# A trunk layer with planned side work: w_ada streamed through the place of keys and values, w_attn_proj sums made where they are used

## The chip, the cores and the metric

The kernel runs on one core of a Trainium2 chip. Its engines are TensorE (PE; its weight loads are listed as PEld), VectorE (DVE), ScalarE (ACT), GpSimd (POOL) and SyncE (SP), which here only issues transfers. Every engine works through its own instructions in order and waits for others through semaphores; transfers run on 16 DMA engines. The metric is the device time of one execution in microseconds, as the median of several runs, and less is better.

## The reference

One layer of a decoder trunk on x (2048 x 1024), float32:

```python
mod = silu(c) @ w_ada + b_ada                    # 3 x 1024: shift, scale, gate
u = x * (1 + scale) + shift
q, k, v, a_gate, p_in, p_gate, m_a, m_p = split(u @ w_in)
a = (sliding_window_gqa_with_sinks(q, k, v, bias) * silu(a_gate)) @ w_attn_proj
p = (group_linear(causal_pool(p_in), w_pool_mix) * pool_scale * silu(p_gate)) @ w_pool_proj
y = ((sigmoid(m_a) * a + sigmoid(m_p) * p) @ w_out) * (1 + gate)
out = layer_norm(alpha * x + y)
```

There are 16 query heads and 2 key heads of 64, a window of 128 and a bias by distance.

## The kernel before, in words

**Products.** A float32 matrix is split into a high half (rounded to the type of one fast pass, ACT) and a low half (the rest, one subtraction, on DVE or POOL: `low`, L124), and `mm3` (L130) multiplies high by high, high by low and low by high. The big products take a 2 x 2 block scheme with seven products instead of eight (`Quad`, L256): both operands need sums of their blocks. On the moving side these are the "sets" B11, T1, T2, B21, T3, B22, T4 and B12, each [128, 4, 2, 512] with high and low halves; on the weight side a quad holds three tiles `W` (L153, two buffers) and one `A22`. `Quad.load` fetches blocks and makes the first sum on POOL (L276), `mid` makes two more (L283, L284) and fetches a block over one that is used up (L285), `late` one more (L292). The eight products of w_attn_proj have their weight sums made ahead, by `weight_sums` (L229) in the second gate phase, into HBM (`wq_d`), and load them from there (`number` is set, L268 to L271, L281, L290).

**Stages.** The 2048 rows go in two halves of 1024. (1) The head (L962 to L1033): w_ada times silu(c) gives shift, scale and gate in `mod`; PE makes shift from `wadat` (`modulation_mm`, L979), DVE makes scale from `wada` by a multiply with a running sum (`modulation`, L954). Tile by tile, x is modulated on ACT and made into sets, and each tile is multiplied into the first two quads' open products. (2) First gate phase: one quad for keys and values and 16 for the four gates (`gate_quads`, L942), two quads to a group. (3) First attention, 64 steps, a head pair and a block of 128 rows each. (4) and (5): the same for the second half. (6) The mixing phases ("mix"): w_attn_proj and w_pool_proj for the first half, both for the second, then w_out with the layer norm.

**What sets the order.** A planner orders instructions on each engine by its own estimate of time; calls through `pe`, `act`, `dve`, `pool`, `sp` (L83) keep the order of the program, all matmuls among them. Side work is hung on "ticks": `ring` (L392) calls the hooks of a tick after every product of 12 matmuls, `steps` (L411) turns a start and offsets into ticks (14 to a group of two quads). Side work of the gate phases: `fold_parts` (L900) multiplies w_pool_mix into a part of w_in, in halves, and stores it for the attention; `sums_to` (L194) fetches two tiles, works on them, stores them and their block sums; in the first gate phase these are the sets of the second half of x, in the second the rows of w_out times 1 + gate. It takes its two tiles from `spare`, a rotation of two 512 KB buffers shared with the folds, with `weight_sums` and with the builds of sets. `bias_rows` (L548) lays out the attention bias with 32 small POOL instructions.

**Ends of attention.** From step 51 the next phase's first two quads are loaded, split (`early_hi`, `early_lo`) and multiplied (`fill_one`, L756) beside the last steps, and its sets are built from `raw` tiles. PSUM has four `mm` banks; two of them hold the last pooled inputs until `pool_diff` (L656) has read them.

## Time and profile before

| what | us |
|---|---|
| median of 3 runs | 1969.79 (1968.75 to 1978.54) |
| profiled execution, its own time | 1969.13 |
| its span | 1967.4 |
| busy: PE, DVE, POOL, ACT | 1763.7, 1321.0, 1020.0, 943.3 |
| granted TensorE clock, mean | 0.961 |

In the profile's rows, `L55` stands for every instruction issued through the ordered engines, so tiles tell more than lines: `mm`, `lg`, `pv`, `pt` are PSUM banks, `w_set` a split weight, `W` and `A` a quad's weight blocks, `sig` a gate, `st_hi` and `st_lo` a fold's result. A row of the timeline gives start, duration, engine, line, operation, output and input; in brackets stands how long the engine had been idle before it and what ended that. A row of the waits names who waited for whom, the total, the times and the longest.

### The profile page before, as it was taken

The page shows a single profiled execution, that of the slowest core. Times are in us where ns is not written, and L with a number is a line of the kernel's source. Part 1 is how long each engine was busy: PE and PEld are TensorE (multiplying, and loading weights), DVE is VectorE, ACT ScalarE, POOL GpSimd, SP SyncE. Part 2 cuts the span into 40 slices and gives each one's busy share as a digit, 9 for nine tenths or more (in the row PEclk, how much of TensorE's full clock was granted, in tenths as well). Part 3 has the DMA queues.
Part 4 walks back from the last instruction along what each step waited for, and adds up shares of the span by engine and source line. Part 5 has one row for each costly group of instructions (what it writes and reads, how often), then busy time and mean ns, then how long its engine had stood idle before and what let it go on. Part 6 is the DMA issues. An engine that isn't in the chain of part 4 may idle for free. (4 is left out here: it accounts for less than half of the span.)

```text
span 1967.4 us, 25174 instructions
## 1 busy us (share of the span) xinstructions
PE 1763.7 (90%) x8248; PEld 1458.6 (74%) x8248; DVE 1321.0 (67%) x2252; ACT 943.3 (48%) x1945; POOL 1020.0 (52%) x908
## 2 busy tenths in 40 slices
PE   4589799989999997887899999999969989988996
PEld 3478687768888886666688888888758768766775
DVE  5565555354687888765544447787867886888776
ACT  2443333333777776422333357777734344333443
POOL 3464746541366777766533314667632751576452
PEclk9789999999999998898899999999979999999998
DMA  6352746366354444565533344444467686675442
GB/s 230 129 203 93 230 149 213 135 218 163 121 162 130 149 157 169 201 208 198 182 102 124 105 137 124 150 150 143 152 216 249 204 279 208 221 237 200 139 140 95
DMA packets 144147, 335.18 MB, mean 170 GB/s; under 512 B 19072, under 2 KB 23184, under 8 KB 144016
## 3 DMA queue, kind: packets, MB, share of 16 engines
q1 hardware_dynamic: 118112, 253.29, 40.3%
q0 software_dynamic: 20512, 67.15, 9.1%
q10 hardware_dynamic: 5392, 13.14, 1.9%
q8 instruction: 65, 1.06, 0.2%
q14 instruction: 66, 0.54, 0.1%
HBM read 224.43 MB, written 112.23 MB: 171 GB/s over the span
## 5 line engine op out<-in xcount | busy, mean ns | idle before, releaser
L55 PE MATMUL mm<-set_B,w_set 128*128 128x512 f32 x3240 | 817.5, 401 | 73.3 <-DVE w_set L125 22.0
L55 PEld LDWEIGHTS mm<-set_B,w_set 128*128 128x128 f32 x3240 | 612.1, 192 | 211.1 <-DVE w_set L125 30.0
L55 PE MATMUL lg<-set_T,w_set 128*128 128x512 f32 x2088 | 529.5, 404 | 77.6 <-DVE w_set L125 40.2
L55 PEld LDWEIGHTS lg<-set_T,w_set 128*128 128x128 f32 x2088 | 401.6, 195 | 179.6 <-DVE w_set L125 50.8
L125 DVE TENSOR_TENSOR w_set<-W,w_set 128x1024 fp32r<-128x1024 f32 x166 | 248.4, 1497 | 164.2 <-ACT w_set L314 149.6
L314 ACT CAST w_set<-W 128x1024 fp32r<-128x1024 f32 x166 | 174.4, 1051 | 278.0 <-PE mm L55 186.0
L55 PE MATMUL mm<-set_T,w_set 128*128 128x512 f32 x1080 | 272.2, 400 | 2.9 <-DVE w_set L55 2.9
L55 PEld LDWEIGHTS mm<-set_T,w_set 128*128 128x128 f32 x1080 | 205.5, 193 | 46.6 <-DVE w_set L55 3.7
L365 POOL TENSOR_TENSOR p<-p,u 128x512 f32<-128x512 f32 x58 | 85.3, 1473 | 157.9 <-DVE u L364 157.6
L292 POOL TENSOR_TENSOR W<-W 128x512 f32<-128x512 f32 x50 | 67.0, 1341 | 149.9 <-DVE w_set L125 138.8
L283 POOL TENSOR_TENSOR W<-W 128x512 f32<-128x512 f32 x50 | 78.1, 1561 | 117.1 <-DVE w_set L125 109.7
L55 ACT ACTIVATE L<-L,nm 128x257 f32<-128x257 f32 (+1 forms) x256 | 127.4, 500 | 10.6 <-DVE nm L55 3.7
L55 DVE TENSOR_TENSOR o<-pv,o 64x128 f32<-64x128 f32 x256 | 72.1, 282 | 77.1 <-ACT o L55 74.4
L55 DVE CUSTOM_DVE_ANT_0 L<-lg,bt,nsink 128x256 f32<-128x256 f32 (+1 forms) x256 | 111.6, 473 | 7.8 <-DMA bt<-e_rep 2.0
L276 POOL TENSOR_TENSOR W<-W,A 128x512 f32<-128x512 f32 x50 | 69.1, 1383 | 72.8 <-DMA W<-in_win_dram 33.9
L55 DVE TENSOR_SCALAR L<-L,sm 128x256 f32<-128x256 f32 (+1 forms) x128 | 97.2, 759 | 0.0
L55 ACT ACTIVATE L<-L,sm 128x256 f32<-128x256 f32 (+1 forms) x128 | 64.4, 503 | 54.0 <-DVE sm L55 53.8
L55 DVE TENSOR_TENSOR ptl<-pt,pth 128x512 fp32r<-128x512 f32 (+1 forms) x128 | 85.6, 669 | 1.5 <-ACT pth L55 1.4
L55 POOL TENSOR_TENSOR w_set<-W,w_set 128x1024 fp32r<-128x1024 f32 x14 | 33.7, 2405 | 98.5 <-ACT w_set L55 65.0
L284 POOL TENSOR_TENSOR W<-W 128x512 f32<-128x512 f32 x50 | 81.2, 1624 | 6.1 <-DMA W<-in_win_dram 3.5
L55 ACT COPY o<-pv 64x256 f32<-64x256 f32 x128 | 47.4, 370 | 76.4 <-PE pv L55 75.4
L125 DVE TENSOR_TENSOR set_T<-spare,set_T 128x1024 fp32r<-128x1024 f32 (+1 forms) x48 | 61.4, 1281 | 31.7 <-ACT set_T L180 31.6
(172 smaller groups left out, 2631.0 us busy)
## 6 DMA issues: line engine op xcount, KB each, us to landing
W<-in_win_dram SPq DMA_DIRECT2D x102, 256.0 KB, 3.4
w_set<-wmix_d SPq DMA_DIRECT2D x32, 512.0 KB, 5.9
A<-in_win_dram SPq DMA_DIRECT2D x34, 256.0 KB, 3.3
wa<-in_wada_dram SPq DMA_DIRECT2D x32, 256.0 KB, 3.8
ag_d<-sig SPq DMA_DIRECT2D x32, 256.0 KB, 3.4
pg_d<-sig SPq DMA_DIRECT2D x32, 256.0 KB, 3.4
ma_d<-sig SPq DMA_DIRECT2D x32, 256.0 KB, 2.4
mp_d<-sig SPq DMA_DIRECT2D x32, 256.0 KB, 2.9
```

The source lines that it names most:

```text
L55: return lambda *args, **kw: self.tc.keep_in_program_order(op(*args, **kw))
L125: engine.tensor_tensor(dst, src, as32(hi), ALU.subtract)
L276: nc.gpsimd.tensor_tensor(x[:, 1, :], x[:, 2, :], self.a22, ALU.add)
L283: nc.gpsimd.tensor_tensor(x[:, 1, :], x[:, 1, :], x[:, 0, :], ALU.subtract)
L284: nc.gpsimd.tensor_tensor(x[:, 2, :], x[:, 0, :], x[:, 2, :], ALU.subtract)
L292: nc.gpsimd.tensor_tensor(x[:, 0, :], x[:, 0, :], x[:, 1, :], ALU.subtract)
L314: nc.scalar.copy(by_two(hi), raw)
L365: nc.gpsimd.tensor_tensor(p5, p5, u2, ALU.add)
```

## The change

- **Head.** `head` and `places` are new. The tiles of `wadat` and `wada` come in one load each, into six places that lie where keys (`kk`) and values (`vv`) will stand later, instead of five half-size buffers. Tiles 0 and 4 are fetched and modulated, then the first two quads' weights; then for each i the sets of tiles i and 4 + i are made, the next two tiles are fetched and modulated, and only then are the products of tile i issued. `bias_rows` runs here instead of at tick 7 of the third group.
- **First gate phase.** `fold_parts` comes in five steps of one tick each (fetch, split, fold and fetch, split, fold), with the low half on DVE instead of POOL. The eight rows of w_ada for the gate come through `spare`, two every 28 ticks, instead of all from tick 92 on.
- **Second gate phase.** `weight_sums` and `wq_d` go; the sums of w_out start at tick 9 + 24.5 i with a stretch of 1.8 instead of 18 + 25.5 i with 1.1; the gate's rows are written in the first group instead of the second.
- **w_attn_proj.** Its quads make their sums on POOL like all others.
- **Attention.** The first low half of the next phase's weights goes to POOL, a step later; T1 is split three steps after its load; the four early products come in the order T1, B11, B11, T1 instead of T1, B11, T1, B11; the last two pool differences come one step earlier.

```diff
     class Quad:
         def load(self, ph, own):
             self.w, self.a22 = ph.weights(), ph.last(own)
-            x, made = self.w, self.number is not None
-            if made:
-                nc.sync.dma_start(x[:, 0, :], self.srcs[0][:, 0:CH])
-                nc.sync.dma_start(x[:, 1, :], wq_d[self.number, 0])
-                nc.sync.dma_start(x[:, 2, :], wq_d[self.number, 2])
-                nc.sync.dma_start(self.a22, self.srcs[1][:, CH:])
-                return
+            x = self.w
...
         def early_lo(x, which):
             hi, lo = pre[x, which]
-            low(dve, by_two(lo), nxt_group[x].first(), by_two(hi))
+            low(dve if x or which else pool, by_two(lo), nxt_group[x].first(), by_two(hi))
...
             if n < 64:
                 if n % 2 == 0:
                     opened.append([bank(), bank(), None, None])
-                    product(opened[x][1], pair(x, 0)[1], "T1", True)
-                else:
-                    product(opened[x][0], pair(x, 0)[0], "B11", True)
+                k = (n - 60) % 3 == 0
+                product(opened[x][k], pair(x, 0)[k], "T1" if k else "B11", True)
...
+            for at, x, which in ((57, 0, 0), (60, 1, 0), (62, 0, 1), (64, 1, 1)):
...
-                if n % U == 5 + 2 * st and (j, st) in sums:
+                if n % U == 4 + (j + 1 < KT) + 2 * st and (j, st) in sums:
                     pl = pool_diff(j, sums.pop((j, st)), accs.pop(("mix", j, st)))
...
             if n in (26, 42):
-                build(ph, "T1", n // 42, nxt_store, eng=(act, pool), raw=ph.weights()[:, 0:2])
+                t1_raw = ph.weights()[:, 0:2]
+                nc.sync.dma_start(t1_raw, nxt_store["T1"][n // 42])
+            if n in (29, 45):
+                split_set("T1", 2 * (n // 45), t1_raw, 2, eng=(act, pool))
...
     def fold_parts(ph, g):
+        m, r, w = [], [], []
+        def fetch(half):
+            if half == 0:
+                r.append(ph.c("mr"))
+                nc.sync.dma_start(r[0], mix[g])
+            r.append(ph.spare())
+            nc.sync.dma_start(r[-1], wpt[g, half])
+        def split(half):
...
+            w[:] = ph.split(), ph.split()
+            nc.scalar.copy(w[0], r[-1])
+            low(nc.vector, w[1], r[-1], w[0])
...
+        return (
+            (0, lambda: fetch(0)),
+            (1, lambda: split(0)),
+            (2, lambda: (fold(0), fetch(1))),
+            (3, lambda: split(1)),
+            (4, lambda: fold(1)),
+        )
...
+    def gate_modulation(ph, m, cb):
+        wa = []
+        def fetch():
+            wa.append(ph.spare())
+            nc.sync.dma_start(wa[0], wada[m])
+        def work():
             nc.vector.tensor_tensor_reduce(
+                wa[0], wa[0], cb, 1.0, mod[:, m : m + 1], ALU.mult, ALU.add, mod[:, m : m + 1]
             )
+        return (0, fetch), (3, work)
...
+    def head(ph, places):
...
+        bias_rows(ph)
         sums = bank("pv")
+        xs = {}
+        def fetch(k):
+            wt, wa = place(), place()
+            nc.sync.dma_start(wt, wadat[k])
+            nc.sync.dma_start(wa, wada[KT + k])
+            if k < 4:
+                xs[k] = (ph.spare(),)
+                nc.sync.dma_start(xs[k][0], xt[0, k])
+            else:
+                xs[k] = ph.p("b21"), ph.p("b22")
+                for h, x in enumerate(xs[k]):
+                    nc.sync.dma_start(x, cols(xt[0, k], h))
+            for i in range(KT):
+                mm(sums[:, k : k + 1], wt[:, i * P : (i + 1) * P], ct[:, i : i + 1], ...)
+            m = KT + k
+            nc.vector.tensor_tensor_reduce(
+                wa, wa, cb, 1.0, mod[:, m : m + 1], ALU.mult, ALU.add, mod[:, m : m + 1]
+            )
...
+            for x in xs[k]:
+                nc.scalar.activation(x, x, AF.Identity, bias=mod[:, k : k + 1], scale=mod[:, m : m + 1])
...
+        fetch(0)
+        fetch(4)
+        for q in groups[0]:
+            q.load(ph, False)
...
+        for i in range(4):
+            make_sets(i)
+            if i + 1 < 4:
+                fetch(i + 1)
+                fetch(i + 5)
             for w, (a, b, _, _) in zip(starts, opened):
                 product(a, w[0], "B11", True, i, i + 1)
                 product(b, w[1], "T1", True, i, i + 1)
...
         for g in range(4):
-            for half, f in enumerate(fold_parts(ph, g)):
-                at(2 * g, 2 * half, f)
+            steps(hooks, groups, 28 * g, fold_parts(ph, g))
...
-        at(2, 7, lambda: bias_rows(ph))
...
         for i in range(8):
-            steps(hooks, groups, 92, [(2.6 * i, lambda i=i: modulation(ph, 2 * KT + i, cb, lambda: ph.c("wa")))])
+            steps(hooks, groups, 28 * (i // 2) + 22 + i % 2, gate_modulation(ph, 2 * KT + i, cb))
...
-        hooks[(1, 2)] = [gate_rows]
+        hooks[(0, 2)] = [gate_rows]
...
-            steps(hooks, groups, 6 + 25.5 * i, weight_sums(ph, (wap[2 * i], wap[2 * i + 1]), i))
...
-                1.1,
+                1.8,
             )
-            steps(hooks, groups, 18 + 25.5 * i, todo)
+            steps(hooks, groups, 9 + 24.5 * i, todo)
...
+    def places():
+        big = kvp.tile([P, 4 * (P + 2 * CH)], F32, tag="kk", name="head_kk")
+        small = kvp.tile([P, 2 * (2 * NB + 1) * P], F32, tag="vv", name="head_vv")
+        return [t[:, i * D : (i + 1) * D] for t, n in ((big, 4), (small, 2)) for i in range(n)]
...
+        started = head(ph, places())
+        kk = kvp.tile([P, 2, 2, P + 2 * CH], F32R, tag="kk", name="kk")
+        vv = kvp.tile([P, 2 * NB + 1, 2, P], F32R, tag="vv", name="vv")
+        q0 = first_phase(ph, *started)
```

162 lines of the change are left out of this document (51 added, 111 removed).

## The prediction

> **What bounds the kernel now.** I read the page first, then the windows by stage, then the timeline of TensorE (PE) at each long wait, and only there the other engines. The page says that PE is the bound, but not everywhere.
>
> ```profile
> span 1967.4 us, 25174 instructions
> PE 1763.7 (90%) x8248; PEld 1458.6 (74%) x8248; DVE 1321.0 (67%) x2252; ACT 943.3 (48%) x1945; POOL 1020.0 (52%) x908
> ```
>
> The next rows cut the span by stage: start and end, length, then busy time and instructions of PE, weight load, DVE, ACT and POOL, then granted clock, DMA share, GB/s. In order: head, first gate phase, first attention, its end, first part of the second gate phase, its rest, end of the second attention, first w_attn_proj phase, first w_pool_proj phase.
>
> ```profile
> 0.00:98.00 98.00, 50.23 (x188) 41.55 (x189) 54.58 (x107) 36.20 (x52) 37.49 (x34) 0.90 0.54 180
> 98.00:490.00 392.00, 360.93 (x1622) 297.32 (x1620) 207.47 (x245) 142.21 (x204) 194.04 (x199) 0.96 0.54 174
> 490.00:735.00 245.00, 239.54 (x1356) 207.44 (x1356) 191.09 (x558) 181.88 (x544) 154.94 (x149) 1.00 0.45 146
> 735.00:792.00 57.00, 43.59 (x200) 34.79 (x199) 49.99 (x92) 37.39 (x87) 40.20 (x37) 0.90 0.53 179
> 792.00:952.00 160.00, 124.07 (x497) 98.42 (x497) 97.86 (x89) 48.18 (x69) 105.65 (x102) 0.88 0.58 196
> 952.00:1150.00 198.00, 198.00 (x875) 163.93 (x874) 86.97 (x98) 74.22 (x105) 69.83 (x52) 1.00 0.39 132
> 1400.00:1458.00 58.00, 38.07 (x173) 30.23 (x171) 40.07 (x86) 31.20 (x79) 33.27 (x31) 0.84 0.53 181
> 1458.00:1540.00 82.00, 81.11 (x341) 65.50 (x342) 63.09 (x68) 39.25 (x46) 18.91 (x12) 0.97 0.71 236
> 1540.00:1610.00 70.00, 62.71 (x267) 50.07 (x266) 61.05 (x51) 24.87 (x28) 50.63 (x39) 0.98 0.72 229
> ```
>
> From 952 to 1150 nothing but matmuls counts: 198 / 875 = 0.226 us each. The same kind of work from 792 to 952 takes 160 us for 497 of them, which at that pace are 112.5: 47.5 us are lost there, 35.9 as idle time and 11.6 because matmuls run slower after the pauses (clock 0.88), 0.32 us for each us of pause. The head has 47.8 us without PE, the first gate phase 31.1, the two ends of attention 13.4 and 19.9. So there are some 160 us that better placed side work could win, and the change touches each of these places.
>
> **The head.** The diff moves w_ada loads out of five half-size buffers into six full-size ones (16 + 16 loads of 256 KB become 8 + 8 of 512 KB, in the same SP queue), lets modulation of the next tile precede the products of this one, and adds `bias_rows`.
>
> ```profile
> L55 PE MATMUL mm<-set_B,w_set 128*128 128x512 f32 x24 | 14.5, 692 | 32.7 <-ACT set_B L180 18.7 <-DVE set_B L125 7.9 <-ACT w_set L314 4.6
> L125 DVE TENSOR_TENSOR set_B<-spare,set_B 128x512 fp32r<-128x512 f32 x4 | 9.5, 2375 | 3.7 <-ACT set_B L180 3.7
> L125 DVE TENSOR_TENSOR set_T<-b,set_T 128x512 fp32r<-128x512 f32 x4 | 2.7, 679 | 0.0
> GB/s 28 216 224 396 402 385 374 19 0 94 188 271 288 350 303 115 126 264 277 288 14 110 268 159 134 289 243 188 43 196 200 99 203 225 0 3 0 23 191 0
> DMA packets 8964, 17.64 MB, mean 180 GB/s; under 512 B 1536, under 2 KB 1536, under 8 KB 8960
> ...
> u_B<-spare POOLq DMA_DIRECT2D x4, 256.0 KB, 3.7
> 0.00:50.00 50.00, 23.17 (x77) 18.84 (x77) 27.73 (x68) 14.00 (x19) 17.27 (x19) 1.00 0.67 227
> ```
>
> PE's idle time lies in front of products, behind ACT's and DVE's splits (32.7 of 47.8 us), and these wait for loads: the GB/s row (40 slices of 2.45 us) shows bursts near 400 and holes near zero, so loads wait for buffers, not for bandwidth. 17.64 MB at 402 GB/s are 44 us, at the 227 of the first 50 us 78. DVE, busy 54.6 us, starts its splits when the first tiles are down, five slices or 12 us in, so 67 is an engine floor. I take 73, between floor and slow rate: **-25** (bounds -15 and -35; nothing if the chain of load, modulation and split stays serial). `bias_rows` on POOL (6.1 us, below) falls where POOL waits for the first loads; without that cover the head is 6 us longer.
>
> **The first gate phase.** Three things leave PE's path: the low half of each fold moves from POOL to DVE and one or two ticks ahead of its matmuls; `bias_rows` leaves; the gate rows of w_ada no longer come at once near its end (8 loads of 512 KB spread out for 16 of 256).
>
> ```profile
> PE pv L55 <- POOL w_set L125: 10.8, 7, 2.6
> 228.86 6.06 POOL L561 TENSOR_SCALAR et<-rel 16x1 f32<-16x1 f32 x32
> 239.41 0.79 PE L55 MATMUL mm<-set_B,w_set 128*128 128x512 f32 x1 [6.32 <-DVE w_set L125]
> 422.53 1.04 ACT L314 CAST w_set<-W 128x1024 fp32r<-128x1024 f32 x1 [4.88 <-DMA W<-in_win_dram]
> 423.63 0.80 PE L55 MATMUL lg<-set_T,w_set 128*128 128x512 f32 x1 [6.13 <-ACT w_set L314]
> 134.13 5.40 PE L55 MATMUL lg<-set_T,w_set 128*128 128x512 f32 x12 [4.26 <-DVE p L376]
> ```
>
> The fold waits are 10.8 in all; the 6.06 us of bias rows stand ahead of the weight sum that PE misses at 239 (6.3); at 423 a weight load lands late among the w_ada loads (6.1). After each of the last two the clock costs 2.0 more (0.32 x 6.2; the row at 134 shows the kind, 12 matmuls in 5.40 instead of 2.72). Sum 10.8 + 8.3 + 8.1 = 27. Against it, gate rows are now fetched into the two `spare` buffers right behind the last store of `sums_to`, four times: the SP queue can stand up to the 3.7 us of such a store, with weight loads behind it. Bounds 0 and +15; I take +6, somewhat under half a store each, since weight loads come some ticks ahead of their use. **-21.** The wait at 134, DVE on the keys, stays.
>
> **The second gate phase.** `weight_sums` goes: 12 loads on SP, 16 subtractions and 16 stores on POOL. The sums of w_out start at tick 9 instead of 18 and are stretched from 1.1 to 1.8 ticks.
>
> ```profile
> 813.63 1.65 PE L55 MATMUL lg<-set_T,w_set 128*128 128x512 f32 x3 [6.46 <-DVE w_set L125]
> 861.94 1.62 PE L55 MATMUL lg<-set_T,w_set 128*128 128x512 f32 x3 [7.08 <-DVE p L376]
> 900.64 1.65 PE L55 MATMUL lg<-set_T,w_set 128*128 128x512 f32 x3 [9.44 <-DVE w_set L125]
> ...
> 947.58 1.65 PE L55 MATMUL lg<-set_T,w_set 128*128 128x512 f32 x3 [4.01 <-DVE w_set L125]
> 896.12 1.23 DVE L1093 TENSOR_TENSOR spare<-spare,cb 128x1024 f32<-128x1024 f32 x1 [12.80 <-DMA spare<-in_wout_dram]
> 936.41 5.28 SPq L1083 DMA_DIRECT2D spare<-in_wout_dram  x3
> 941.25 1.04 ACT L314 CAST w_set<-W 128x1024 fp32r<-128x1024 f32 x1 [9.23 <-DMA W<-in_win_dram]
> ```
>
> Each wait has one root: w_out wants the two spare buffers that weight sums still hold. SP stands 5.28 us in three w_out loads, a weight load beside them lands for 941; DVE stands 12.8 us in front of its multiply with p and w_set behind it. Without weight sums the buffers are free at tick 9 and the multiply comes 3.6 ticks (of 12 matmuls, 2.72 us) after its load. The nearest row is the first gate phase, which has the same `sums_to` at 1.7: what it loses outside fold, bias and w_ada is the wait at 134 with its clock, 7 us, and crumbs of 3. So of 47.5 us some 12 stay, the one at 813 (keys again) among them: **-35** (bounds -25 and -43). The gate row on ACT's queue moves to tick 2, ahead of the multiply at tick 12; its cost is nothing as ACT is busy 48 of 160 us.
>
> **The w_attn_proj phases.** Eight quads make their sums on POOL.
>
> ```profile
> L292 POOL TENSOR_TENSOR W<-W 128x512 f32<-128x512 f32 x50 | 67.0, 1341 | 149.9 <-DVE w_set L125 138.8
> L283 POOL TENSOR_TENSOR W<-W 128x512 f32<-128x512 f32 x50 | 78.1, 1561 | 117.1 <-DVE w_set L125 109.7
> L276 POOL TENSOR_TENSOR W<-W,A 128x512 f32<-128x512 f32 x50 | 69.1, 1383 | 72.8 <-DMA W<-in_win_dram 33.9
> L284 POOL TENSOR_TENSOR W<-W 128x512 f32<-128x512 f32 x50 | 81.2, 1624 | 6.1 <-DMA W<-in_win_dram 3.5
> ```
>
> That is 5.9 us a quad, 47 in all, and 16 loads less on SP. POOL is busy 18.9 of 82 us there and takes it. Bounds: 0 (the clean gate quads from 952 on make the same sums at no wait) and 7 us a phase (the w_pool_proj phase, which makes them beside more POOL work). DVE is nearer to the second: **+3** for both.
>
> **The ends of attention.**
>
> ```profile
> 765.90 1.65 PE L55 MATMUL mm<-set_B,w_set 128*128 128x512 f32 x3 [4.78 <-DVE pl L55]
> 1430.96 1.65 PE L55 MATMUL mm<-set_B,w_set 128*128 128x512 f32 x3 [5.28 <-DVE pl L55]
> 1457.95 1.65 PE L55 MATMUL mm<-set_B,w_set 128*128 128x512 f32 x3 [7.82 <-ACT u L355]
> 1446.54 1.76 POOL L55 TENSOR_TENSOR a<-o,ag 128x512 f32<-128x512 f32 x1 [6.82 <-DVE o L55]
> 1455.10 0.56 POOL L192 DMA_DIRECT2D ain_T<-a  x1 [0.30 <-POOL a L55]
> ```
>
> The product of step 62 takes a bank that the last pool difference frees only in step 63. Afterwards step 62 takes the other bank and the difference comes a step earlier: 4.8 and 5.3 go, with 1.6 us of clock each. What is late next is DVE, busy 50 of 57 us in the first end, so I count **-5** there, helped by one low half that moves to POOL. In the second end POOL gets six sums of w_attn_proj (6 x 1.5 us by the rows above) and that low half beside its 33 of 58; its last chain (1446.5 to 1455.7, then a store, then the wait of 7.82) starts with DVE, not POOL, so it stays. **-3** (bounds -8 and +8). Splitting T1 three steps later costs nothing: PE idles 5.5 of 245 us in the steps before 735, so no load is late there.
>
> **Sum.** -25 - 21 - 35 - 5 - 3 + 3 = -86. The profiled execution took 1969.13 us (its span and 1.7 around it), 0.7 below the median of the three runs: 1883.
>
> The Trainium skill ("SBUF — State Buffer", Who interferes with whom) says that a DVE instruction with two SBUF inputs and a GpSimd instruction that reads SBUF exclude each other for the whole instruction. By that rule the moved sums block DVE too; the trace agrees (a 128x512 subtraction takes 2375 or 679 ns in the head), and in full it would make rival 1's time of this sum.
>
> **Rivals.** (1) DVE becomes the bound in the w_attn_proj phases: it has 19 us free in 82, sixteen sums of 1.48 us take 24 if each holds it up in full, 5 too many a phase: 1883 - 3 + 10 = 1890. For it speak 2375 against 679 ns; against it the clean rows after 952. (2) New waits on the two spare buffers take the place of the old: a wait as at 861 (7.1, with clock 9.3) at each of the four hand-overs of the first gate phase, and the head gains its least: 1883 + 37 - 6 + 10 = 1924. (3) The other side: w_attn_proj sums late for all three splits of each of four pairs of quads. A late pair costs 6.7 on average (the four waits above) and a third more of clock: 12 x 8.9 = 107, so 1883 - 3 + 107 = 1987, slower. It decides from 7.5 us a place (90 / 12); the w_pool_proj phase, with such sums, loses 7.3 us in all its 70. (4) The change does not do what it says: the planner puts loads back into the old order and the gain falls to a quarter: 1969 - 21 = 1948. For it, SP's order is the planner's; against it, buffers set these waits, and the diff changes buffers.
>
> **How the numbers follow.** 0.5% (10 us) is about what a measurement of this kernel tells from no change. Forecast or rival 1 (1860 to 1908): 0.60; better, with the head at its floor and both ends in full (below 1860): 0.08; rival 2 (to 1940): 0.16; rival 4 (to 1959): 0.05; within 0.5%: 0.03; rival 3: 0.08. Faster 0.89, slower 0.08. The range 1852 to 1935 leaves out rivals 3 and 4, no change, and the tails of rival 2 and of the best case: 0.08 + 0.05 + 0.03 + 0.04.
>
> **What would show it.** Right: the first gate phase starts near 73 us; no POOL w_set in front of PE pv; no wait over 5 us in the second gate phase but the one behind the keys; no PE wait on pl at the ends; PE above 97% in the w_attn_proj phases. Wrong: SP standing in w_ada loads with W behind them, DVE at 9 tenths in those phases, or a head that still ends above 85 us.

## The result, and the profile after

The changed kernel takes 1953.56 us (median of 5 runs, 1951.16 to 1958.07), the kernel before 1969.79 beside it (5 runs): a ratio of 0.9911, with a 95% interval of 0.9885 to 0.9938. It is faster by 0.9%, more than the 0.5% that a measurement tells from no change, but the forecast was 1883 with a range of 1852 to 1935. Of 86 us some 16 came.

The line of busy times on the page of the kernel after: PE's share of the span did not move, and its work is the same.

```profile
PE 1767.0 (90%) x8248; PEld 1457.9 (75%) x8248; DVE 1332.4 (68%) x2226; ACT 940.2 (48%) x1945; POOL 1036.4 (53%) x902
```

To see where the time went, both profiled executions are cut at the same products: the head ends with the first `lg` product, a gate phase with the first score product of attention, an attention with its last value product. Columns as in the prediction: start and end, length, busy time (instructions) of PE, weight load, DVE, ACT, POOL, then granted clock, DMA share, GB/s. Windows of the kernel before: head, first gate phase, first attention, second gate phase, second attention, rest.

```profile
0.00:89.97 89.97, 46.63 (x176) 39.10 (x177) 48.84 (x101) 31.30 (x44) 31.21 (x31) 0.91 0.57 190
89.97:489.45 399.48, 363.98 (x1631) 299.36 (x1630) 213.21 (x250) 146.75 (x211) 200.32 (x203) 0.96 0.53 172
489.45:778.10 288.65, 273.27 (x1517) 234.88 (x1515) 227.23 (x636) 210.91 (x618) 184.62 (x176) 0.98 0.45 145
778.10:1153.20 375.10, 335.68 (x1427) 272.73 (x1426) 199.28 (x200) 131.12 (x188) 186.00 (x162) 0.95 0.49 167
1153.20:1442.84 289.64, 276.28 (x1549) 239.04 (x1547) 230.40 (x636) 214.99 (x617) 173.74 (x161) 0.98 0.44 141
1442.84:1967.40 524.56, 467.88 (x1959) 373.49 (x1957) 402.00 (x431) 208.25 (x268) 244.11 (x176) 0.96 0.59 199
```

The same windows of the kernel after; the last row is the first w_attn_proj phase alone.

```profile
0.00:85.45 85.45, 43.45 (x176) 37.68 (x176) 49.78 (x91) 34.12 (x50) 45.63 (x66) 0.89 0.68 239
85.45:480.50 395.05, 366.51 (x1629) 298.44 (x1629) 222.08 (x237) 142.62 (x206) 174.23 (x159) 0.96 0.51 172
480.50:773.10 292.60, 274.84 (x1516) 236.03 (x1515) 225.13 (x635) 210.09 (x617) 186.98 (x177) 0.98 0.42 135
773.10:1126.32 353.22, 334.72 (x1428) 272.62 (x1427) 195.91 (x200) 131.47 (x188) 160.67 (x130) 0.97 0.45 153
1126.32:1424.88 298.56, 278.21 (x1549) 239.16 (x1547) 222.42 (x635) 214.24 (x617) 185.47 (x169) 0.98 0.41 132
1424.88:1954.60 529.72, 469.26 (x1958) 374.02 (x1957) 417.10 (x431) 207.68 (x268) 283.38 (x201) 0.95 0.56 188
1439.00:1521.00 82.00, 79.75 (x343) 64.79 (x343) 67.72 (x69) 38.92 (x46) 32.32 (x20) 0.98 0.66 217
```

| stage | forecast | measured |
|---|---|---|
| head | -25 | -4.5 |
| first gate phase | -21 | -4.4 |
| first attention (its end) | -5 | +3.9 |
| second gate phase | -35 | -21.9 |
| second attention (its end) | -3 | +8.9 |
| rest (w_attn_proj) | +3 | +5.2 |
| sum | -86 | -12.8 (1967.4 to 1954.6) |

Only the second gate phase gave most of what was expected; the two attentions, which should have gained a little, lost 12.9 together. The prediction ended the head at 98 us, where the first `lg` product of the kernel before is done (98.45; in the kernel after, 90.77). By that cut 7.7 of the 9.0 us won up to the first attention belong to the head and 1.3 to the gate phase. Some stages scatter between kernels that share all their code: the first gate phase came out between 392.6 (ends_back, below) and 398.3 (late_sums), the head of one code between 77.4 and 79.1. So a difference of 3 us in the one, or of 1.5 us in the other, says nothing.

PE's timeline of the kernel after, at the waits that are left (start, duration, what, in brackets the idle time before it and who ended it).

```profile
85.45 5.32 PE L55 MATMUL lg<-set_T,w_set 128*128 128x512 f32 x12 [4.60 <-ACT w_set L272]
...
190.93 0.73 PE L55 MATMUL lg<-set_T,w_set 128*128 128x512 f32 x2 [0.95 <-ACT w_set L272]
192.19 2.60 PE L55 MATMUL lg<-set_T,w_set 128*128 128x512 f32 x10 [0.52 <-DVE w_set L123]
...
223.08 4.58 PE L55 MATMUL lg<-set_T,w_set 128*128 128x512 f32 x12 [4.19 <-DVE p L334]
...
414.53 5.89 PE L55 MATMUL lg<-set_T,w_set 128*128 128x512 f32 x12 [3.21 <-ACT w_set L272]
...
865.58 4.63 PE L55 MATMUL mm<-set_B,w_set 128*128 128x512 f32 x10 [4.66 <-DVE w_set L123]
...
1371.89 0.58 PE L55 MATMUL pv<-pth,vv 128*128 128x256 f32 x1 [6.83 <-ACT pth L55]
...
1438.68 2.93 PE L55 MATMUL mm<-set_B,w_set 128*128 128x512 f32 x6 [9.32 <-ACT u L313]
```

The bias wait at 239 and the late weight load at 423 of the kernel before are gone (the wait that is left at 414.53 has another origin, below), and so is every wait above 5 us in the second gate phase. New are pairs of short waits on `w_set` around each fold (190.93 and 192.19 are one pair; eight pairs, 11.8 us in all), waits in front of `lg` (4.19), waits of value products for `pth` (6.83), and the wait for the last `u` has grown from 7.82 to 9.32.

### The profile page after: what moved, and what is told of

Its sections match the earlier page's. It is cut to its first block, busy times and chain, and to the rows that moved or that the text cites. A ratio compares the mean times of both kernels' runs of the same rounds, so it can differ in the third digit from the quotient of the medians.

```text
span 1954.6 us, 25013 instructions
## 1 busy us (share of the span) xinstructions
PE 1767.0 (90%) x8248; PEld 1457.9 (75%) x8248; DVE 1332.4 (68%) x2226; ACT 940.2 (48%) x1945; POOL 1036.4 (53%) x902
## 5 line engine op out<-in xcount | busy, mean ns | idle before, releaser
L55 PE MATMUL lg<-set_T,w_set 128*128 128x512 f32 x2088 | 535.9, 407 | 69.1 <-DVE w_set L123 31.6
L123 DVE TENSOR_TENSOR w_set<-W,w_set 128x1024 fp32r<-128x1024 f32 x166 | 238.8, 1438 | 168.8 <-ACT w_set L272 164.7
L250 POOL TENSOR_TENSOR W<-W 128x512 f32<-128x512 f32 x58 | 79.6, 1373 | 177.3 <-DVE w_set L123 167.0
L244 POOL TENSOR_TENSOR W<-W 128x512 f32<-128x512 f32 x58 | 95.9, 1654 | 146.6 <-DVE w_set L123 130.6
L240 POOL TENSOR_TENSOR W<-W,A 128x512 f32<-128x512 f32 x58 | 85.6, 1475 | 63.1 <-DMA W<-in_win_dram 20.9
L245 POOL TENSOR_TENSOR W<-W 128x512 f32<-128x512 f32 x58 | 93.4, 1611 | 9.9 <-DMA W<-in_win_dram 3.8
L55 POOL TENSOR_TENSOR w_set<-W,w_set 128x1024 fp32r<-128x1024 f32 x16 | 38.4, 2402 | 102.4 <-ACT w_set L55 69.3
L55 PE MATMUL pv<-pth,vv 128*128 128x256 f32 x248 | 69.6, 297 | 25.5 <-ACT pth L55 21.7
L123 DVE TENSOR_TENSOR w_set<-A,w_set 128x512 fp32r<-128x512 f32 x58 | 86.1, 1516 | 5.4 <-ACT w_set L279 5.3
L123 DVE TENSOR_TENSOR set_T<-spare,set_T 128x1024 fp32r<-128x1024 f32 (+1 forms) x48 | 67.0, 1398 | 32.8 <-ACT set_T L178 32.5
L55 DVE TENSOR_SCALAR L<-L,sm 128x256 f32<-128x256 f32 (+1 forms) x128 | 87.6, 684 | 0.0
```

What stands on the lines that cost most here:

```text
L55: return lambda *args, **kw: self.tc.keep_in_program_order(op(*args, **kw))
L123: engine.tensor_tensor(dst, src, as32(hi), ALU.subtract)
L240: nc.gpsimd.tensor_tensor(x[:, 1, :], x[:, 2, :], self.a22, ALU.add)
L244: nc.gpsimd.tensor_tensor(x[:, 1, :], x[:, 1, :], x[:, 0, :], ALU.subtract)
L245: nc.gpsimd.tensor_tensor(x[:, 2, :], x[:, 0, :], x[:, 2, :], ALU.subtract)
L250: nc.gpsimd.tensor_tensor(x[:, 0, :], x[:, 0, :], x[:, 1, :], ALU.subtract)
```

## Experiments

Each kernel is the one after with the edit shown, unless another is named. Ratios are to the kernel before, which was measured again beside each group of runs (medians of 1969.8 to 1972.2), so a difference of 2 or 3 us between the medians of two kernels says little.

### The head

Three views of the kernel after. SyncE's wait in front of the second weight loads, from 0 to 86 us (line, what it waited for, total, count, longest):

```profile
SPq L246 <- POOL W L244: 12.6, 2, 11.3
```

Its queue and ACT's modulation in the timeline:

```profile
22.04 0.36 SPq L969 DMA_DIRECT2D head_kk<-in_wada_dram  x1
33.79 0.33 SPq L246 DMA_DIRECT2D W<-in_win_dram  x1
34.17 0.43 SPq L972 DMA_DIRECT2D spare<-in_xt_dram  x1
...
41.17 1.24 ACT L992 ACTIVATE spare<-spare,mod 128x1024 f32<-128x1024 f32 x1 [10.20 <-DMA spare<-in_xt_dram]
```

The buffers were free, yet tile 1 came late: SP stood in the second weight load of `mid` (L246) until POOL had read the buffer that it overwrites (L244), and the loads of tile 1 stood behind it in the same queue. The modulation of tile 0 began at 12.93, that of tile 1 28 us later.

**mid_later**: the second half of the weight loads goes behind the fetch of the next tiles.

```diff
         starts = [pair_split(ph, q.first()) for q in groups[0]]
-        for q in groups[0]:
-            q.mid()
...
                 fetch(i + 5)
+            if i == 0:
+                for q in groups[0]:
+                    q.mid()
```

> The changed kernel with the mid step of the first two quads (their POOL sums and the second W load) after the loads of tiles 1 and 5. Theory A: SP stands 12.6 us in those second W loads behind POOL's sums, with the loads of tile 1 behind it; moved behind them, tile 1 is modulated some 10 us earlier (ACT's second modulation of spare at 41.2 comes near 31) and the first lg product falls from 85.45 to 75 to 79: total 1943 to 1947. Theory B: the head is bound by its chain of load, modulation and splits on DVE whatever SP does; the first lg product stays at 83 to 87 and the total within 3 us of 1953.6.

**bias_back**: `bias_rows` goes back to tick 7 of the third group.

```diff
         nc.vector.tensor_tensor(cb, cb, cg, ALU.mult)
-        bias_rows(ph)
...
+        at(2, 7, lambda: bias_rows(ph))
```

> The changed kernel with bias_rows back at tick 7 of the third group of the first gate phase. Theory A: what bias_rows releases in the head, eight e_rep loads of 384 KB, holds SP up there (12.0 us of SP waits name e_rep), so the head's last product (first lg product, at 85.45 us in the changed kernel) comes 5 to 10 us earlier, while the first gate phase (395.1 us from there to the first attention) gets back a wait of 6 to 8 us on DVE behind POOL: total 1945 to 1956, a gain or nothing. Theory B, that of the prediction: bias_rows is hidden in the head, so the first lg product stays within 2 us of 85.45 and the gate phase is 6 to 8 us longer: 1959 to 1962.

**head2**: both edits.

> The mid step later (as in mid_later, first lg product at 78.04 us) and bias_rows back in the gate phase (as in bias_back) together. Theory A: two things held tile 1's loads, one behind the other, the second W loads and the e_rep loads (SP waits of 17.7 us in mid_later's head name e_rep): the first lg product comes at 68 to 73, the gate phase is 6 us longer: total 1945 to 1952. Theory B: behind the W loads the head is bound by DVE's splits and reductions; the lg product stays at 76 to 79, and the total is 1953 to 1958.

Measured: mid_later 1950.03 us (0.9896 [0.9877, 0.9915]), its head 78.04, 7.4 less; bias_back 1959.64 (0.9952 [0.9937, 0.9967]), its head 84.39, first gate phase 401.6; head2 1956.61 (0.9917 [0.9893, 0.9940]), head 77.47, first gate phase 404.0. PE's timeline of bias_back:

```profile
235.71 4.63 PE L55 MATMUL mm<-set_B,w_set 128*128 128x512 f32 x10 [5.29 <-DVE w_set L123]
```

SP's order was the largest single loss in the head, and its 7.4 us are in the range that the queue theory gave for the head (75 to 79), though only 3.5 of them reach the median and its range for the total was missed. `bias_rows` at tick 7 brings the wait at 239 back, at 235.71, and the phase is 6.6 longer: that term of the prediction (8.3) was right in kind and nearly in size, and the cover in the head holds (1.1 us at most).

What holds the head at 77 or 78? Two more kernels, both on **best2** (below), ask whether it is the loads or PSUM. **late_spread** issues the eight `e_rep` loads (the attention bias, which `bias_rows` makes ready) on SP in the program's order instead of on ACT's queue, so that they come in the gate phase (216 to 391 us) and not in the head; **two_banks** does that and puts the modulation sums into two PSUM banks.

```diff
-        nc.scalar.dma_start(e_rep[:, 2 * j : 2 * j + 2, :], e_d[2 * j : 2 * j + 2, :].partition_broadcast(P))
+        sp.dma_start(e_rep[:, 2 * j : 2 * j + 2, :], e_d[2 * j : 2 * j + 2, :].partition_broadcast(P))
...
-        sums = bank("pv")
+        sums = [bank("pv"), bank("pt")]
...
-                    sums[:, k : k + 1],
+                    sums[k // 4][:, k : k + 1],
```

> best2 with the eight e_rep loads issued on SP in the order of the program, so that they stay in the first gate phase and leave the head; bias_rows itself stays in the head. Theory A: the slots that they take hold SP in the head (17.7 us of waits in mid_later name e_rep): the first lg product falls from 78 or 79 to 70 to 75, total 4 to 8 below best2. Theory B: they only stand where SP would wait for places anyway; the lg product stays within 2 us, total within 3 of best2.

> late_spread with the modulation sums of tiles 0 to 3 and 4 to 7 in two PSUM banks in place of one. Theory A: PE's modulation products of the next tile stand behind DVE's read of the bank (in head2 three waits of 8.4, 4.7 and 5.8 us name it), and DVE reads it behind a row of splits: with two banks the lg product falls by another 4 to 8 us, total 4 to 8 below late_spread. Theory B: DVE's splits and reductions, some 13 to 15 us a pair of tiles, bound the head; the lg product stays within 2 us of late_spread.

Measured: late_spread 1916.40 us (0.9726 [0.9704, 0.9749]), head 77.35 for 78.82 in best2; two_banks 1917.92 (0.9732 [0.9710, 0.9755]), head 76.52. SP's waits in late_spread:

```profile
SPq L246 <- POOL W L244: 16.7, 2, 14.9
```

PE's timeline of two_banks, at the modulation of tile 2:

```profile
41.26 3.54 PE L55 MATMUL pv<-ct,head_kk 128*128 128x1 f32 x16 [7.51 <-DMA head_kk<-in_wadat_dram]
```

The waits on `e_rep` went, and SP now stands 14.9 us at the weight load behind POOL instead (15.1 in two_banks). Waits of PE for the bank (8.35, 5.29 and 5.14 us in late_spread) went too, and in their place PE waits 7.51 us for a `wadat` load and 4.6 us in front of `mm`. Neither step of the head, 1.5 and 0.8 us, is larger than its scatter: mid_later, best1, best2 and fold_same, whose head has the same code, end it at 78.04, 79.13, 78.82 and 77.38. So each wait that was removed uncovered another. What sets the 77 is open: SP still stands at the weight load with the next tiles' loads behind it, and DVE, busy 56.9 of the first 80 us in two_banks, has the reductions and splits of each pair of tiles to do; no run takes the loads out of the way.

### The fold

The change draws each fold out over five ticks, with the split one tick ahead of its products. The rotation `w_set` has four buffers, that is two pairs of high and low halves, and a pair that is split a tick early is held a tick longer. **fold_back** puts the whole fold back as before, POOL's low half included; **fold_only** keeps the change's five parts, DVE's low half included, but splits in the tick of the products.

```diff
             (0, lambda: fetch(0)),
-            (1, lambda: split(0)),
-            (2, lambda: (fold(0), fetch(1))),
-            (3, lambda: split(1)),
-            (4, lambda: fold(1)),
+            (2, lambda: (split(0), fold(0), fetch(1))),
+            (4, lambda: (split(1), fold(1))),
```

> The changed kernel with fold_parts as before (split in the tick of its matmuls, low half on POOL). Theory A: the split a tick ahead holds two of the four w_set buffers, so the next pair is split late; what it won in front of pv (10.8 us) it pays in front of lg (16 short waits, 11.8 us). Undone, the short waits go, those of pv on POOL come back, and the first gate phase stays within 3 us of 395.1: total 1951 to 1957. Theory B, that of the prediction: the move won what it took away, so the phase is 9 to 12 us longer: 1962 to 1966.

> The changed kernel with each fold's split in the tick of its matmuls and nothing else. Theory A: the low half on DVE wins, and the tick ahead gave it back: the first gate phase falls from 395.1 to 384 to 390, total 1942 to 1949. Theory B: in the changed kernel DVE is held by POOL's sums in these ticks, so the split comes late and PE waits in front of pv: phase 393 to 398, total within 3 us of 1953.6.

Measured: fold_back 1958.16 us (0.9944 [0.9923, 0.9966]), first gate phase 394.4; fold_only 1945.52 (0.9859 [0.9839, 0.9880]), first gate phase 381.6. PE's timeline of fold_back:

```profile
101.41 0.50 PE L55 MATMUL pv<-mhi,w_set 128*128 128x256 f32 x2 [1.93 <-POOL w_set L123]
```

The window of fold_only:

```profile
86.29:467.88 381.59, 359.28 (x1628) 293.23 (x1629) 219.81 (x237) 142.50 (x206) 176.50 (x159) 0.99 0.53 178
```

With the old fold the short pairs are gone and POOL's waits are back (10.9 us in seven waits), at the same length of the phase: one was exchanged for the other. With the split in its tick both are gone, but for one wait of 1.4 to 1.6 at each of the four folds: 13.5 us less than after (6.2 of idle time, and 7.2 of busy time at a clock of 0.99 for 0.96), 8.0 in the median. The prediction's fold term, 10.8, was to be had; the tick ahead gave it back. Not all of the 13.5 is the short pairs, though: the waits on `p` of the next section shrink here too.

### DVE behind POOL

PE's waits at 223 and 315 end with DVE's `p`, which stands behind low halves that last far too long. DVE and POOL of the kernel after, in the timeline (start, duration):

```profile
212.47 6.83 DVE L123 TENSOR_TENSOR w_set<-A,w_set 128x512 fp32r<-128x512 f32 x2
...
212.98 1.31 POOL L240 TENSOR_TENSOR W<-W,A 128x512 f32<-128x512 f32 x1
214.96 1.30 POOL L245 TENSOR_TENSOR W<-W 128x512 f32<-128x512 f32 x1
216.20 1.29 POOL L202 TENSOR_TENSOR spare<-spare 128x512 f32<-128x512 f32 x1
217.45 1.29 POOL L240 TENSOR_TENSOR W<-W,A 128x512 f32<-128x512 f32 x1
219.29 1.27 POOL L245 TENSOR_TENSOR W<-W 128x512 f32<-128x512 f32 x1
```

The same two halves in the kernel before:

```profile
216.96 1.31 DVE L125 TENSOR_TENSOR w_set<-A,w_set 128x512 fp32r<-128x512 f32 x2
```

Two halves of 0.65 us take 6.83 beside a row of POOL's subtractions and sums. **no_subs** leaves the 32 subtractions of `sums_to` out; **subs_dve** has them on DVE; **gatemod_back** brings the gate rows of w_ada back to tick 92, through the half-size buffers, to see whether the new use of `spare` makes the waits (rival 2).

```diff
-            nc.gpsimd.tensor_tensor(x(*out), x(*a), x(*c), ALU.subtract)
+            nc.vector.tensor_tensor(x(*out), x(*a), x(*c), ALU.subtract)
```
```diff
-            steps(hooks, groups, 28 * (i // 2) + 22 + i % 2, gate_modulation(ph, 2 * KT + i, cb))
+            steps(hooks, groups, 92, [(2.6 * i, lambda i=i: modulation(ph, 2 * KT + i, cb, lambda: ph.c("wa")))])
```

> The changed kernel with the four block subtractions on POOL in each sums_to left out (32 in all, the stores stay, so part of the computation is missing). Theory A: the waits of the gate phases that are left (4.2 at 223 and 315 in the first; 2.5, 4.7 and 2.1 at 853, 865 and 901 in the second) come from DVE's low halves standing still while POOL works through a row of sums without a gap (two halves of A in 6.83 us at 212, where the same two took 1.31 before): without the 32 sums those two take under 2 us, the waits at 223 and 315 are under 1, and the two phases together lose 15 to 25 us (395.1 + 353.2 to 724 to 733): total 1929 to 1939. Theory B: these waits come from late loads and buffers; they stay within 1 us and the total within 4 us of 1953.6.

> The changed kernel with those 32 subtractions on DVE in place of POOL; nothing left out. Theory A: DVE has the room (226 of 395 us busy) and does one in about 0.7 us where POOL takes 1.3; with POOL's row broken up, the low halves of A take under 3 us the pair and the waits at 223 and 315 fall under 2: the phases lose 8 to 20 us, total 1934 to 1946. Theory B: DVE's queue is what PE waits for; 2.7 us more in each round make the waits longer: total 1955 to 1965.

> The changed kernel with the gate rows of w_ada again at ticks 92 to 110 in 16 half loads through the c buffers. Theory A, that of the prediction: spreading them took away the wait at 423 (6.1 us and 2 of clock); as the spread rows still cost 3.2 us and 3 of clock at 414, the undone phase is 1 to 4 us longer than 395.1: total 1954 to 1958. Theory B: the rows fetched into the spare buffers push the folds and sums behind them, and so make the waits at 223 and 315; undone these fall under 1.5 us and the phase to 386 to 391: total 1945 to 1950.

Measured: no_subs 1952.19 us (0.9894 [0.9876, 0.9912]); subs_dve 1942.03 (0.9841 [0.9820, 0.9862]), first gate phase 387.4 and second 346.1; gatemod_back 1956.79 (0.9916 [0.9896, 0.9936]), first gate phase 398.2. The groups of the first gate phase by form, for the low halves from `A` (count, busy, mean ns), in the kernel after:

```profile
L123 DVE TENSOR_TENSOR w_set<-A,w_set 128x512 fp32r<-128x512 f32 x17 | 31.2, 1873 | 2.9 <-ACT w_set L279 2.9
```

in no_subs:

```profile
L123 DVE TENSOR_TENSOR w_set<-A,w_set 128x512 fp32r<-128x512 f32 x17 | 15.0, 917 | 2.5 <-ACT w_set L278 2.5
```

and in subs_dve:

```profile
L123 DVE TENSOR_TENSOR w_set<-A,w_set 128x512 fp32r<-128x512 f32 x17 | 20.0, 1210 | 1.5 <-ACT w_set L279 1.5
```

The mechanism holds: the mean goes from 1873 ns to 917 without the subtractions and to 1210 with them on DVE (1171 in the kernel before, which has them on POOL), and the waits at 223 and 315 go. It matters which of POOL's rows the low halves meet: in fold_only, with the subtractions on POOL, two such halves at 205.60 take 3.18 us, and PE has no wait above 0.5 us on `p` but the one behind the keys. The Trainium skill ("SBUF — State Buffer", Who interferes with whom) says that a DVE instruction with two SBUF inputs and a GpSimd instruction that reads SBUF exclude each other; the trace agrees, by these means. The rule stood in the prediction, but for the w_attn_proj phases alone.

The total of no_subs did not follow (the theory gave 1929 to 1939). Its second gate phase is 345.2, as short as in subs_dve, but its first is 398.8, at the upper end of the scatter, with new waits. PE's timeline of no_subs and one of DVE's rows just ahead:

```profile
207.44 1.28 DVE L934 CUSTOM_DVE_ANT_0 spare<-spare,cb,mod 128x1024 f32<-128x1024 f32 x1 [2.01 <-DMA spare<-in_wada_dram]
...
213.50 4.64 PE L55 MATMUL lg<-set_T,w_set 128*128 128x512 f32 x10 [4.80 <-DVE w_set L123]
```

Without the subtractions the `spare` buffers come free earlier, the gate rows and fold loads in them move too, and DVE stands at a reduction (2.01) with the low half behind it. How much of the lost gain this explains was not measured. In gatemod_back PE's timeline shows that the waits on `p` stay without gate rows in `spare`:

```profile
316.10 5.28 PE L55 MATMUL lg<-set_T,w_set 128*128 128x512 f32 x12 [4.19 <-DVE p L334]
...
417.25 4.19 PE L55 MATMUL lg<-set_T,w_set 128*128 128x512 f32 x8 [4.39 <-ACT w_set L272]
```

So the use of `spare` is not their cause. The wait of 4.39 is not the one of the kernel before at 423, where ACT stood for a weight load. It is the wait of 3.21 that the kernel after has at 414.53, and both begin at DVE, which stands in front of a reduction of w_ada with `u`, ACT's gate and the split behind it. DVE in the kernel after and in gatemod_back:

```profile
410.85 1.28 DVE L935 CUSTOM_DVE_ANT_0 spare<-spare,cb,mod 128x1024 f32<-128x1024 f32 x1 [6.14 <-DMA spare<-in_wada_dram]
...
414.18 0.75 DVE L931 CUSTOM_DVE_ANT_0 wa<-wa,cb,mod 128x512 f32<-128x512 f32 x1 [7.91 <-DMA wa<-in_wada_dram]
```

The late weight load did not come back with the gate rows. The phase is 3.2 longer, within its scatter, and so is the median, with overlapping intervals: the spreading is worth 3 us or nothing, not 8.1.

### Attention: T1, and the ends

**t1_back** splits T1 with its load again, not three steps later. **ends_back** does that and also undoes the four edits at the ends (the low half on POOL, the step later, the order of the early products, the earlier pool difference).

```diff
             if n in (26, 42):
                 t1_raw = ph.weights()[:, 0:2]
                 nc.sync.dma_start(t1_raw, nxt_store["T1"][n // 42])
-            if n in (29, 45):
-                split_set("T1", 2 * (n // 45), t1_raw, 2, eng=(act, pool))
+                split_set("T1", 2 * (n // 42), t1_raw, 2, eng=(act, pool))
```
```diff
-            low(dve if x or which else pool, by_two(lo), nxt_group[x].first(), by_two(hi))
+            low(dve, by_two(lo), nxt_group[x].first(), by_two(hi))
...
-                k = (n - 60) % 3 == 0
-                product(opened[x][k], pair(x, 0)[k], "T1" if k else "B11", True)
+                    product(opened[x][1], pair(x, 0)[1], "T1", True)
+                else:
+                    product(opened[x][0], pair(x, 0)[0], "B11", True)
...
-                if n % U == 4 + (j + 1 < KT) + 2 * st and (j, st) in sums:
+                if n % U == 5 + 2 * st and (j, st) in sums:
```

> The changed kernel with the splits of T1 back at steps 26 and 42 in both attentions, right behind their loads. Theory A: the low half of T1 on POOL (2.41 us), now at step 45, pushes POOL's queue back in steps 45 to 57, so that pl, of one buffer, is held and PE waits on pth (4.34 us at 720, 6.83 at 1372); back at step 42 each of these waits shrinks by 2.4 us or more, and the stages (292.6 and 298.6 us) by 2 to 5 each: total 1944 to 1950. Theory B: those waits come from the w_attn_proj sums and from the edits at the ends; they stay within 1 us, and the total within 3 us of 1953.6.

> t1_back (1944.79) with the other edits of the ends undone as well: early halves at 56 with both low halves on DVE and behind the other work of the step, the old order of banks, the last pool difference at 5 + 2 st. The w_attn_proj sums at their use stay. Theory A, that of the prediction: these edits win 5 and 3 us: the waits on pl (4.8 and 5.3) come back, the stages go from 287.4 and 292.6 to 292 and 296, total 1951 to 1955. Theory B: they only trade waits on pl for waits on pth: stages within 1.5 us, total within 3 us of 1944.8.

Measured: t1_back 1944.79 us (0.9873 [0.9856, 0.9890]), first attention 287.4 for 292.6, second 292.6 for 298.6; ends_back 1941.27 (0.9841 [0.9821, 0.9861]), 286.3 and 291.3. POOL's half of T1 and what follows it, in the timeline of the kernel after:

```profile
1322.28 2.41 POOL L55 TENSOR_TENSOR set_T<-W,set_T 128x1024 fp32r<-128x1024 f32 x1
...
1368.63 1.26 POOL L55 TENSOR_TENSOR p<-pl,pg 128x512 f32<-128x512 f32 x1
1369.93 0.69 DVE L55 SCALAR_TENSOR_TENSOR pl<-nxt,mm 128x512 f32<-128x512 f32 x1 [8.84 <-POOL p L55]
```

In the timeline of t1_back, the value product that waited 6.83:

```profile
1358.22 0.58 PE L55 MATMUL pv<-pth,vv 128*128 128x256 f32 x1 [2.76 <-ACT pth L55]
```

The step that the prediction costed at nothing costs 11.1 us in the two attentions and 8.8 in the median. The split's POOL half, 2.4 us, stands three steps later in POOL's queue; POOL's `p` comes late, DVE stands 8.84 us for it (4.74 in t1_back), and the value product waits for `pth`. More than the half moves: the raw T1 tile takes one of the two `W` buffers, and the first weight load of the next phase waits for its split. SP's wait in the kernel after, from 1290 to 1350 us:

```profile
SPq L237 <- POOL set_T L55: 3.0, 1, 3.0
```

In t1_back that wait is as long (3.4) but 11.8 us earlier in the stage, so two weight sums of 1.29 us on POOL move along with the half. How much of the loss is the half, how much the sums and the load is not separated; 46 us of POOL's queue, with pauses, lie between the split and the late `p`. That PE idled only 5.5 of 245 us before 735 said how things stood with the old place of the split, not with the new one.

In ends_back the two waits that the end edits were made of come back in PE's timeline:

```profile
751.40 4.38 PE L55 MATMUL mm<-set_B,w_set 128*128 128x512 f32 x12 [4.78 <-DVE pl L55]
...
1396.21 4.08 PE L55 MATMUL mm<-set_B,w_set 128*128 128x512 f32 x10 [4.77 <-DVE pl L55]
```

and still it is not slower than t1_back: 3.5 us less in the median, 1.1 and 1.3 in the stages. The two intervals overlap a little, and best1, with the same attention code, has 288.4 and 291.5, so the sign is likely rather than sure. The waits for `pth` shrink (4.6 to 2.0 us in all in the first attention, 7.3 to 3.9 in the second) and the last wait for `u` goes from 8.89 to 6.96. The edits removed the waits they were aimed at and moved them.

### The second gate phase and w_attn_proj

**late_sums** gives the sums of w_out their old place and stretch, with weight sums still gone. **wsums_back** does that and brings `weight_sums`, `wq_d` and the numbered quads back.

```diff
-                1.8,
+                1.1,
             )
-            steps(hooks, groups, 9 + 24.5 * i, todo)
+            steps(hooks, groups, 18 + 25.5 * i, todo)
```
```diff
+            steps(hooks, groups, 6 + 25.5 * i, weight_sums(ph, (wap[2 * i], wap[2 * i + 1]), i))
```

> The changed kernel with the sums of w_out at their old ticks (18 + 25.5 i, stretch 1.1), still without weight_sums. Theory A, that of the prediction: the root was weight_sums holding the two spare buffers; without it the old ticks lose little more: second gate phase 353 to 359 us (353.2 in the changed kernel, 375.1 before), total 1953 to 1960. Theory B: half or more of what was won is the wider spacing of the sums on POOL and of load and multiply: phase 364 to 372, total 1964 to 1972.

> The changed kernel with weight_sums, the quads that read its results, and the old ticks of the sums of w_out. Both theories: second gate phase back near 375 us. Theory A: making the w_attn_proj sums at their use costs more than the +3 forecast, since six of them fall into the second end of attention: without them the second attention falls from 298.6 to 291 to 294 and the rest behind it from 514.7 to 509 to 511: total 1962 to 1968. Theory B: the T1 split alone makes the second attention long; it stays at 297 to 299 and the rest at 512 to 515: total 1972 to 1978.

Measured: late_sums 1959.63 us (0.9935 [0.9915, 0.9955]), second gate phase 354.9 for 353.2; wsums_back 1967.46 (0.9976 [0.9961, 0.9991]), second gate phase 373.4. Windows of wsums_back: second gate phase, second attention, rest.

```profile
770.62:1144.01 373.39, 335.76 (x1427) 273.07 (x1426) 203.93 (x200) 131.15 (x188) 186.25 (x162) 0.95 0.49 167
1144.01:1436.89 292.88, 279.27 (x1548) 240.64 (x1547) 226.56 (x635) 214.42 (x617) 175.49 (x162) 0.98 0.43 139
1436.89:1958.80 521.91, 464.58 (x1959) 371.23 (x1957) 404.73 (x431) 207.93 (x268) 241.16 (x176) 0.96 0.60 200
```

SP's wait in the second gate phase of wsums_back, in front of the loads of w_out:

```profile
SPq L1118 <- DMA wq_d<-spare: 23.0, 9, 4.1
```

The two differ by the weight sums and by the quads that read them. The weight sums cost the second gate phase 18.5 us (373.4 to 354.9), and the place and stretch of the other sums matter little (1.7). That they do it by holding the spare buffers is what SP's wait for their stores says; in late_sums they wait only for the stores of the sums before them. But their 16 subtractions on POOL go as well, and the mean of the low halves from `A` falls from 1136 to 850 ns, so the two ways are not separated. The sums made where they are used cost 4.4 in the second attention and 8.2 in the rest up to the last product (515.3 to 507.1); against the kernel before, the rest lost 5.2. The profiled execution of wsums_back is the fastest of its ten, 6.9 us under their median, so these sizes are rough. By the medians, 1967.46 to 1959.63, 7.8 of the gain is left.

### Put together

**best1** is the kernel after with t1_back, the end edits undone and mid_later; **best2** adds subs_dve; **fold_same** adds the fold split in its tick.

> The changed kernel with three things together: T1 split back at steps 26 and 42, the edits of the ends undone (as in ends_back, 1941.27), and the mid step behind the loads of tile 1 (as in mid_later, head 7 us shorter). If the parts add up: 1934 to 1938. If the shorter head only runs into waits that stood behind it (mid_later itself gained 3.5 of its 7.4 in the median): 1938 to 1941.

> best1 (1936.69) with the 32 subtractions of sums_to on DVE. If the gain of subs_dve (11.5 us in the median) adds to best1: 1923 to 1928. If the waits it removed are partly the same as those that best1 removed: 1929 to 1934.

> best2 with each fold's split in the tick of its matmuls, low half still on DVE. Theory A: the short waits (16 of 0.9 and 0.5 us in front of lg, 11.8 in all) come from the third pair of w_set held a tick ahead; they go, and in their place PE waits in front of pv for the split, about 1.2 to 2.3 us (ACT and DVE, one behind the other) eight times: the first gate phase within 5 us of best2's, either way. Theory B: the short waits have another cause and stay.

Measured: best1 1936.69 us (0.9818 [0.9798, 0.9839]); best2 1917.22 (0.9727 [0.9701, 0.9752]); fold_same 1910.83 (0.9694 [0.9675, 0.9713]). The window of the first gate phase in fold_same:

```profile
77.38:454.68 377.30, 358.50 (x1629) 294.20 (x1629) 221.94 (x253) 142.46 (x206) 155.10 (x143) 0.98 0.53 180
```

best1 is the sum of its parts (1934 to 1938 worked out from them), best2 is 6 us better than the sum (1923 to 1928). fold_same is 6.4 us under best2, and its first gate phase 7.6 shorter (377.3 for 384.9), more than the 5 that its theory allowed. It is the fastest of all, 3.1% under the kernel before and 2.2% under the kernel after, whose two gate phases take 395.1 and 353.2 us to its 377.3 and 345.1.

## Why the prediction was right or wrong

The direction was right, and of the waits in its list most went where it said. Six terms were mis-sized, all to the same side.

- **Head, -25, got -4.5** (-7.7 by the prediction's own cut). The steps "I take 73" and "loads wait for buffers" failed. The buffers were freed, but the loads of tile 1 then waited in SP's queue behind weight loads that wait for POOL: 7.4 us by mid_later. The case that the prediction had in a bracket, the chain that stays serial, was most of it, and its own sign of being wrong, a head that ends above 85 us, came (85.45). "67 is an engine floor" came from DVE's busy time and its first start; no run came below 76.5, and whether loads or DVE hold it there is open. `bias_rows` lies under cover as forecast.
- **First gate phase, -21, got -4.4.** Bias was right (6.6 for 8.3). The fold term, 10.8, failed in the step "one or two ticks ahead of its matmuls", counted as free: with a pair held a tick longer PE waits 11.8 in short pairs; without it the phase gains 13.5 more. The gate rows were worth 3 or nothing, not 8.1. And the new low halves on DVE land beside POOL's row of subtractions, which wasn't in the sum at all.
- **Second gate phase, -35, got -21.9.** That the weight sums were the root was right (18.5 by wsums_back against late_sums), and the spare buffers at least a part of the way. The step "the nearest row is the first gate phase" was too good: low halves on DVE still stand behind POOL's subtractions, and with these moved the phase takes 346.1, 29 below the kernel before.
- **w_attn_proj, +3, got +5 to +8** in the rest. The step took the two w_attn_proj phases alone; in the first it was near (PE busy 79.75 of 82, 97%, against 81.11); where in the rest the others went was not traced. Another 4.4 went in the second attention, whose POOL has the first six sums beside its own chain. The prediction saw these six and set them at nothing in its term for the second end, -3.
- **T1, 0, got +11.1** in the two attentions, the dearest step of all for its size. The working looked at PE's idle time before the move, where POOL's queue and the `W` buffer had to be followed after it.
- **Ends, -8, got nothing** (2.4 us the wrong way in the two stages, 3.5 in the median, near the scatter). The waits on `pl` went and came back as waits on `pth` and on the last `u`.

Of the rivals, 2 named new waits on spare buffers. The new waits of 4.2 are not theirs, as gatemod_back shows; at the last hand-over one came in small, SP standing 6.0 us for a store out of `spare` in front of a w_ada load. Rival 1, DVE as the bound of the w_attn_proj phases, did not come, though its mechanism, DVE held by POOL, cost time in both gate phases. Rival 3, the w_attn_proj sums late, asked for 107; these sums cost at most 12.6 (8.2 and 4.4), and whether PE waited for late ones was not traced. Rival 4 is nearest in number (1948), by luck: its mechanism, loads kept in an order that undoes the gain, holds for the head alone.

## What to carry to other kernels

A step that is moved must be costed on the queue that it lands in, not by PE's idle time at the old place: T1's split, 2.4 us on POOL, cost 11 when it moved three steps, and SP's weight load in front of tile 1 cost 7. Work made a tick earlier holds its buffer a tick longer; where a rotation has four buffers, two pairs, count them before calling it free. DVE instructions with two inputs in SBUF should not share a stretch with a gapless row on POOL, and giving that row to DVE can be cheaper than leaving the two beside each other.

## What the runs showed of the hardware that was not expected

- How strongly the exclusion works: two low halves of 0.65 us each lasted 6.83 us, while POOL's five instructions beside them kept their 1.3. POOL paused from 214.29 to 214.96 and from 218.74 to 219.29, to issue a store; the first half ended at 214.85 and the second at 219.30: it looks as if DVE comes in only in POOL's pauses. That is a reading of one place.
- In mid_later SP's waits name `e_rep` loads of ACT's queue, with which the waiting load shares no buffer (7.0, 6.3 and 4.4 us). In late_spread, where the `e_rep` loads come after the head and on SP, these waits are gone; no run has them in the head on another queue. Why a load on one queue waits for another queue's was not found.
- Waits of PE for a PSUM bank, of 8.35, 5.29 and 5.14 us by their records, went when the bank was no longer shared, and the head ended 0.8 us earlier, within its scatter, since PE then stood 7.51 us for a load: a wait that the records name isn't yet a cost, on PE either.
